# Two unmerged gate units of a feed-forward block become merged ones: predicted and tested

## The chip, the cores and the metric

The program runs on one core of one Trainium2 chip. The core has five engines that run side by side, each through its own list of instructions in a fixed order: TensorE (PE: matrix products, with weight loads, PEld, that overlap them), VectorE (DVE), ScalarE (ACT), GpSimd (POOL) and SyncE (SP, which issues DMAs). An instruction that has to wait for another engine holds up everything behind it on its own engine. The metric is the device time of one execution in microseconds; less is better.

## The reference

One layer: a modulated input goes through a token mixer (windowed attention and retention, gated and projected), a layer norm, and then through the part that the change is in, a feed-forward block with a short convolution over the 256 tokens. All in float32, sequence 256, width 1024, hidden width 2816:

```python
def conv_ffn(h, w_ff_gate, w_ff_up, ff_conv_w, ff_conv_b, w_ff_down):
    s = h.shape[1]
    g = h @ w_ff_gate
    u = h @ w_ff_up
    gp = jnp.pad(g, ((0, 0), (CONV_WIDTH - 1, 0), (0, 0)))
    g_conv = sum(gp[:, j:j + s, :] * ff_conv_w[j] for j in range(CONV_WIDTH)) + ff_conv_b
    a = jax.nn.gelu(g_conv, approximate=False) * u
    return a @ w_ff_down
```

A second layer norm follows.

## The kernel before, in words

**Precision.** A float32 value is split in two parts, hi and lo, and a product is the sum of three: hi by hi, hi by lo, lo by hi. A weight unit is 128x2048 float32, loaded by one DMA into one of four `raw` buffers and split in two halves of 128x1024: ScalarE casts a half into `whi` (L1338), VectorE subtracts (L1352) and gives `wlo`; eight buffers each. The DMA for a later unit waits until the subtraction has read the `raw` buffer.

**Steps.** The main part is a list of steps, two per weight unit as a rule, whose order is that in which the units are written down. At each step the builder emits the splits of the halves that come some halves later, then whatever was put off to this step (`put_off(n, ...)` means n steps later), and then the step's own products and what follows them at once. So the order on every engine is fixed when the program is built.

**The feed-forward block.** The hidden width is cut into 11 rounds of 256. The up products of rounds 0 and 1 are made first, in one group with tokens on the partitions; they are copied to `u4` (L795), transposed on TensorE into banks 6 and 7 (L800, called by `first` in the middle of gate 0) and copied to `uT` (L801). Then come the units gate 0, gate 1, gate 2, up 2, down 0, down 1, gate 3, up 3, down 2, gate 4, and so on. A gate or up unit gives 256 hidden columns of 256 tokens, as two halves of 128 columns. There are two kinds:

- *Unmerged* (`wstat8`, gates 0 and 1): per half 8 k-tiles by three products of 256 columns (L123, L124, L125), both halves in one PSUM bank of 512 columns, which sums all three. `gate_done` then runs once per unit: first taps with the bias on ScalarE (L814, twice), the other two taps on VectorE straight from PSUM (L817, four times), Gelu (L819), and at once `act_in`: product with up (L860) and the split of the result into hi and lo (L100, L101), which are the operands of the down unit.
- *Merged* (`wstat8m`, all others): h's hi and lo parts lie side by side, so that one product of 512 columns (L134) does whi by both, and one of 256 (L138) does wlo by hi. Each half has a bank of its own. The bank's two column halves have to be added afterwards: ScalarE copies the second to an SBUF slot (L489), and one step later VectorE adds the first to it (L492). The bank is free after that addition. For a gate all three taps follow on VectorE from SBUF (L836, then L838 twice), and Gelu one step later (L841). For an up the product with the gate follows (L848) and the split one and two steps later.

**Banks.** There are eight PSUM banks, P0 to P7. Gate and up units take the next of P0 to P3 in turn (`one_bank`). The down units sum in P4 to P7 until the end.

**Order inside a merged unit.** The first step makes 8 products of 512 into the first bank, then the first product of 512 into the second bank, then 8 of 256 into the first bank. The second step makes 8 of 256 and 7 of 512 into the second bank.

## Time and profile before

| what | value |
|---|---|
| median of 3 runs | 421.58 us (421.49 to 421.66) |
| the profiled execution | 421.43 us |
| its span, first to last instruction | 419.7 us |
| TensorE, matrix products | 412.5 us busy, 98% of the span |
| VectorE | 368.1 us, 88% |
| ScalarE | 248.5 us, 59% |
| mean granted TensorE clock | 0.997 |

The execution takes 1.7 us more than its span. Rows of the timeline give start and length in us of instructions or of runs of equal ones (xN), and in brackets how long the engine stood idle before and what ended that. The length of a run goes from the start of its first to the end of its last; on ScalarE and VectorE an instruction starts about 0.1 us before the one ahead of it ends, so the distance of two starts is what an instruction costs its engine in a run. In the chain of waits the end of the program is followed back from instruction to instruction through what released each.

### The profile page before, as it was taken

The page shows a single profiled execution, that of the slowest core. Times are in us where ns is not written, and L with a number is a line of the kernel's source. Part 1 is how long each engine was busy: PE and PEld are TensorE (multiplying, and loading weights), DVE is VectorE, ACT ScalarE, POOL GpSimd, SP SyncE. Part 2 cuts the span into 40 slices and gives each one's busy share as a digit, 9 for nine tenths or more (in the row PEclk, how much of TensorE's full clock was granted, in tenths as well). Part 3 has the DMA queues.
Part 4 walks back from the last instruction along what each step waited for, and adds up shares of the span by engine and source line. Part 5 has one row for each costly group of instructions (what it writes and reads, how often), then busy time and mean ns, then how long its engine had stood idle before and what let it go on. Part 6 is the DMA issues. An engine that isn't in the chain of part 4 may idle for free.

```text
span 419.7 us, 5879 instructions
## 1 busy us (share of the span) xinstructions
PE 412.5 (98%) x2140; PEld 348.1 (83%) x2140; DVE 368.1 (88%) x597; ACT 248.5 (59%) x410; POOL 14.0 (3%) x26
## 2 busy tenths in 40 slices
PE   7999999999999999999999999999999999999995
PEld 4888888888878888888888898888888888888884
DVE  6889799969998889899887987999999888789996
ACT  5666568787955587535544886555555545455700
POOL 0000000100001000001000001000000010003200
PEclk9999999999999999999999999999999999999998
DMA  8998997685688768789662094985866777450002
GB/s 298 405 410 328 414 404 302 247 324 208 222 308 328 254 244 346 304 319 341 223 269 101 1 361 169 373 295 189 307 260 215 281 284 242 187 198 2 1 6 97
DMA packets 18541, 105.60 MB, mean 252 GB/s; under 512 B 2256, under 2 KB 3536, under 8 KB 7760
## 3 DMA queue, kind: packets, MB, share of 16 engines
q1 hardware_dynamic: 16992, 99.70, 63.1%
q0 software_dynamic: 1376, 4.99, 3.5%
q10 hardware_dynamic: 144, 0.52, 0.5%
q8 instruction: 17, 0.28, 0.3%
q14 instruction: 12, 0.10, 0.1%
HBM read 104.15 MB, written 1.06 MB: 251 GB/s over the span
## 4 chain that ended last, share of the span: by engine, by line
PE 97%; DVE 1%; DMA 1%; issue 0%; DVEq 0%; ACT 0%; ACTq 0%
PE P L134 19%; PE P L123 15%; PE P L124 15%; PE P L125 15%; PE P L329 13%; PE P L138 10%; DMA raw<-in_m 1%; PE P L731 1%; PE P L734 1%; PE P L733 1%; PE P L1125 1%; PE P L1231 1%; PE P L1147 1%; PE P L1171 1%; DVE unread L266 1%; PE P L675 0%
## 5 line engine op out<-in xcount | busy, mean ns | idle before, releaser
L1352 DVE TENSOR_TENSOR wlo<-raw,whi 128x1024 fp32r<-128x1024 f32 x118 | 141.9, 1220 | 14.0 <-ACT whi L1338 13.8
L1338 ACT ACTIVATE whi<-raw 128x1024 fp32r<-128x1024 f32 x118 | 122.1, 1056 | 39.3 <-DMA raw<-in_wpr 10.6
L123 PE MATMUL P<-whi,AH 128*128 128x512 f32 x128 | 50.6, 395 | 0.0
L125 PE MATMUL P<-whi,AH 128*128 128x512 f32 x128 | 49.9, 390 | 0.0
L124 PE MATMUL P<-wlo,AH 128*128 128x512 f32 x128 | 49.8, 389 | 0.0
L329 PE MATMUL P<-whi,AH 128*128 128x512 f32 x160 | 41.7, 391 | 1.1 <-DVE AH L295 1.1
L134 PE MATMUL P<-AYa,whi 128*128 128x512 f32 x144 | 41.7, 391 | 0.0
L255 DVE CUSTOM_DVE_ANT_0 junk<-raw,srow 128x1024 bf16<-128x1024 f32 x32 | 39.0, 1219 | 0.0
L134 PE MATMUL P<-AYb,whi 128*128 128x512 f32 x144 | 38.7, 390 | 0.0
L329 PEld LDWEIGHTS P<-whi,AH 128*128 128x128 f32 x160 | 29.8, 188 | 8.4 <-ACT whi L312 1.9
L489 ACT ACTIVATE A<-P 128x256 f32<-128x256 f32 x36 | 13.7, 381 | 33.9 <-PE P L138 23.6
L134 PEld LDWEIGHTS P<-AYb,whi 128*128 128x128 f32 x144 | 27.0, 188 | 6.0
L312 ACT ACTIVATE whi<-raw 128x512 fp32r<-128x512 f32 (+1 forms) x26 | 20.8, 824 | 17.7 <-DMA raw<-in_b 16.3
L134 PEld LDWEIGHTS P<-AYa,whi 128*128 128x128 f32 x144 | 25.8, 189 | 4.2
L315 DVE TENSOR_TENSOR wlo<-raw,whi 128x512 fp32r<-128x512 f32 (+1 forms) x26 | 23.5, 936 | 6.2 <-ACT whi L312 5.8
L123 PEld LDWEIGHTS P<-whi,AH 128*128 128x128 f32 x128 | 24.0, 188 | 5.2 <-issue 0.3
L125 PEld LDWEIGHTS P<-whi,AH 128*128 128x128 f32 x128 | 24.0, 188 | 5.1
L124 PEld LDWEIGHTS P<-wlo,AH 128*128 128x128 f32 x128 | 24.1, 188 | 4.8
L329 PE MATMUL P<-wlo,AH 128*128 128x512 f32 x80 | 23.2, 390 | 0.0
L138 PE MATMUL P<-AYb,wlo 128*128 128x256 f32 x144 | 23.1, 283 | 0.0
L138 PE MATMUL P<-AYa,wlo 128*128 128x256 f32 x144 | 23.0, 282 | 0.0
L138 PEld LDWEIGHTS P<-AYa,wlo 128*128 128x128 f32 x144 | 20.9, 190 | 1.4
(323 smaller groups left out, 776.1 us busy)
## 6 DMA issues: line engine op xcount, KB each, us to landing
raw<-in_ada SPq DMA_DIRECT2D x16, 1024.0 KB, 5.1
raw<-in_wup SPq DMA_DIRECT2D x11, 1024.0 KB, 5.7
raw<-in_wgate SPq DMA_DIRECT2D x11, 1024.0 KB, 5.7
raw<-in_wdown SPq DMA_DIRECT2D x11, 1024.0 KB, 4.9
raw<-in_winB SPq DMA_DIRECT2D x6, 1024.0 KB, 6.8
raw<-in_m SPq DMA_DIRECT2D x4, 1024.0 KB, 8.3
raw<-in_b SPq DMA_DIRECT2D x4, 1024.0 KB, 7.2
raw<-in_wrot SPq DMA_DIRECT2D x4, 1024.0 KB, 7.4
```

Of the source, the lines that this page charges most:

```text
L123: pe.matmul(o, lh, rh, start=start, stop=False)
L124: pe.matmul(o, lh, rl, start=False, stop=False)
L125: pe.matmul(o, ll, rh, start=False, stop=stop)
L134: pe.matmul(banks()[half], t[0][:, k * 128:(k + 1) * 128], x2(k), start=k == 0, stop=half > 0 and k == 7)
L138: pe.matmul(banks()[half][:, :256], t[1][:, k * 128:(k + 1) * 128], x2(k)[:, 0], start=False, stop=half == 0 and k == 7)
L255: dve.tensor_tensor_reduce(out=nobody(j if own else None), in0=raw, in1=srow, scale=1.0, scalar=0.0, op0=OP.mult, op1=OP.add, accum_out=mo ...
L312: act.activation(hi[:, o], raw[:, o], AF.Copy)
L315: dve.tensor_tensor(lo[:, o], raw[:, o], f(hi[:, o]), OP.subtract)
L329: pe.matmul(pa[b0 + c // 512 * 2 + t], x[xi][:, j, t * 128:(t + 1) * 128], ws[k][:, c:c + 512], start=first and (xi, k) == (0, 0), stop=la ...
L489: act.activation(t, p[:, 256:], AF.Copy)
L1338: act.activation(hi, src, AF.Copy)
L1352: dve.tensor_tensor(lo, src, f(hi), OP.subtract)
```

## The change

Gates 0 and 1 become merged units, and the unmerged kind goes. What follows differs a little from the other merged gates: the first tap of the first half is made on ScalarE (from the SBUF slot, L806 in the changed kernel), and the other two taps of that half are put off one step. The product with up and the split (`act_in`) are put off two steps after the second half's taps, and Gelu one step. The transposes of `uT` stay between the two halves of gate 0. The line that set the bank counter back to 0 inside gate 0 goes.

```diff
-MERGED = 2
+XROWS = 2
-    def merged(src, x2, done):
+    def merged(src, x2, done, mid=None):
...
         def two(ts):
+            if mid:
+                mid()
             low(ts[0], 1)
             high(ts[0], 1, range(1, 8))
             done(1, banks()[1])
...
-    def wstat8(name, u, xh, xl, done, mid=None):
...
-    def gate_done(r):
...
     def gate_done_m(r):
         def fn(half):
             g, x = gu(r)[:, half], gu(r)[:, 2 + half]
             convw = consts["convw"]
             w = lambda n: convw[:, n, 2 * r + half:2 * r + half + 1]
-            dve.tensor_scalar(g, x, w(2), w(3), op0=OP.mult, op1=OP.add)
-            for n in (1, 0):
-                dve.scalar_tensor_tensor(g[:, 2 - n:], x[:, :254 + n], w(n), g[:, 2 - n:],
-                                         op0=OP.mult, op1=OP.add)
+            early = r < XROWS and half == 0
+            if early:
+                act.activation(g, x, AF.Identity, scale=w(2), bias=w(3))
+            else:
+                dve.tensor_scalar(g, x, w(2), w(3), op0=OP.mult, op1=OP.add)
+
+            def taps():
+                for n in (1, 0):
+                    dve.scalar_tensor_tensor(g[:, 2 - n:], x[:, :254 + n], w(n), g[:, 2 - n:],
+                                             op0=OP.mult, op1=OP.add)
+            if early:
+                put_off(1, taps)
+            else:
+                taps()
             if half:
                 put_off(1, lambda: act.activation(gu(r)[:, :2], gu(r)[:, :2], AF.Gelu))
+                if r < XROWS:
+                    put_off(2, lambda: act_in(r))
         return fn
...
-    def act_in(r, u):
...
+    def act_in(r):
+        g = gu(r)[:, :2]
+        dve.tensor_tensor(g, S["uT"][:, 2 * r:2 * r + 2], g, OP.mult)
+        ah, al = S["a", r] = a_slots(r)
+        split(ah, al, g)
...
     def first():
-        bank_i[0] = 0
         for t in range(2):
             up_T(t)
 
-    wstat8("wgate", 0, gh2, gl2, gate_done(0), first)
+    ffn_gate(0, first)
     ffn_gate(1)
```

How the instructions stand on three engines, in lists that give line, operation, output and operands. The number behind a tile's name is that of its allocation, so that P3_2270 is bank 3 as gate 0 uses it and P3_2398 the same bank as gate 2 uses it; A5 and A15 are the slots of the rounds in turn; raw_2203 is the unit down 0, raw_2211 down 1, raw_2251 gate 3.

ScalarE before, from the last cast of up 2 on. The first cast of down 0 (from raw_2203) is followed by the copies to uT, gate 0's taps and Gelu, the hi part of the result (A9a), and only then the other halves of down 0 and down 1:

```order
L1338 ACTIVATE whi_2253<-raw_2026 128x1024
L1338 ACTIVATE whi_2294<-raw_2203 128x1024
L801 ACTIVATE AH_2193<-P6_2298 128x4x128
L801 ACTIVATE AH_2193<-P7_2304 128x4x128
L814 ACTIVATE A5_2334<-P2_2269,tables_592 128x256 x2
L819 ACTIVATE A5_2334<-A5_2334 128x512
L100 ACTIVATE A9a_2343<-A5_2334 128x512
L1338 ACTIVATE whi_2347<-raw_2203 128x1024
L1338 ACTIVATE whi_2378<-raw_2211 128x1024
```

ScalarE now, from the same place to the Gelu of gate 0:

```order
L1307 ACTIVATE whi_2253<-raw_2026 128x1024
L475 ACTIVATE A5_2288<-P2_2269 128x256
L1307 ACTIVATE whi_2290<-raw_2203 128x1024
L806 ACTIVATE A5_2288<-A5_2288,tables_592 128x256
L787 ACTIVATE AH_2193<-P6_2296 128x4x128
L787 ACTIVATE AH_2193<-P7_2302 128x4x128
L475 ACTIVATE A5_2288<-P3_2270 128x256
L1307 ACTIVATE whi_2324<-raw_2203 128x1024
L475 ACTIVATE A15_2355<-P0_2336 128x256
L1307 ACTIVATE whi_2357<-raw_2211 128x1024
L819 ACTIVATE A5_2288<-A5_2288 128x512
```

The tap of gate 0's first half (L806) now stands ahead of the two uT copies, of the copy of gate 0's second half and of the cast of down 0's second half; it reads what VectorE's addition writes.

VectorE before, from the first subtraction of down 0 on; the taps read the banks themselves:

```order
L1352 TENSOR_TENSOR wlo_2296<-raw_2203,whi_2294 128x1024
L817 SCALAR_TENSOR_TENSOR A5_2334<-P2_2269,tables_592,A5_2334 128x255 x2
L817 SCALAR_TENSOR_TENSOR A5_2334<-P2_2269,tables_592,A5_2334 128x254 x2
L860 TENSOR_TENSOR A5_2334<-AH_2193,A5_2334 128x512
L101 TENSOR_TENSOR A2a_2344<-A5_2334,A9a_2343 128x512
L1352 TENSOR_TENSOR wlo_2349<-raw_2203,whi_2347 128x1024
L1352 TENSOR_TENSOR wlo_2380<-raw_2211,whi_2378 128x1024
```

VectorE now, from the same place to the first addition of gate 1:

```order
L1321 TENSOR_TENSOR wlo_2292<-raw_2203,whi_2290 128x1024
L478 TENSOR_TENSOR A5_2288<-P2_2269,A5_2288 128x256
L1321 TENSOR_TENSOR wlo_2326<-raw_2203,whi_2324 128x1024
L812 SCALAR_TENSOR_TENSOR A5_2288<-A5_2288,tables_592 128x255
L812 SCALAR_TENSOR_TENSOR A5_2288<-A5_2288,tables_592 128x254
L478 TENSOR_TENSOR A5_2288<-P3_2270,A5_2288 128x256
L808 TENSOR_SCALAR A5_2288<-A5_2288,tables_592 128x256
L812 SCALAR_TENSOR_TENSOR A5_2288<-A5_2288,tables_592 128x255
L812 SCALAR_TENSOR_TENSOR A5_2288<-A5_2288,tables_592 128x254
L1321 TENSOR_TENSOR wlo_2359<-raw_2211,whi_2357 128x1024
L478 TENSOR_TENSOR A15_2355<-P0_2336,A15_2355 128x256
```

The subtraction of down 0's second half now stands between the two additions of gate 0. After the last row shown come the second subtraction of down 1, the product with up and the split of gate 0, the two put-off taps of gate 1's first half, and then the addition of its second half.

TensorE now, the end of gate 1, gate 2 and the start of up 2, with what an instruction waits for in brackets:

```order
L134 MATMUL P1_2337<-AYb_1546,whi_2205 128x512 x4
L134 MATMUL P2_2397<-AYa_1545,whi_2241 128x512 [waits DVE_49,Activation_49]
L134 MATMUL P2_2397<-AYa_1545,whi_2241 128x512 x3
L134 MATMUL P2_2397<-AYb_1546,whi_2241 128x512 x4
L134 MATMUL P3_2398<-AYa_1545,whi_2243 128x512 [waits DVE_49,Activation_49]
L138 MATMUL P2_2397<-AYa_1545,wlo_2245 128x256 x4
L134 MATMUL P0_2458<-AYa_1545,whi_2247 128x512 [waits DVE_49,Activation_49]
L134 MATMUL P0_2458<-AYb_1546,whi_2247 128x512 x4
L134 MATMUL P1_2459<-AYa_1545,whi_2253 128x512 [waits DVE_49,Activation_49]
```

Some rows between are left out. Before, gate 0 had P2 alone, gate 1 P0 alone, gate 2 P1 and P2, up 2 P3 and P0; now gate 0 has P2 and P3, gate 1 P0 and P1, gate 2 P2 and P3 again, up 2 P0 and P1 again.

## The prediction

> **What bounds the kernel now.** The first page gives the busy shares and the chain of waits by engine.

> ```profile
> span 419.7 us, 5879 instructions
> PE 412.5 (98%) x2140; PEld 348.1 (83%) x2140; DVE 368.1 (88%) x597; ACT 248.5 (59%) x410; POOL 14.0 (3%) x26
> PE 97%; DVE 1%; DMA 1%; issue 0%; DVEq 0%; ACT 0%; ACTq 0%
> ```

> 97% of the chain is TensorE. So only two things move the end: fewer or shorter products, and a new wait of TensorE. I then cut the time into stages (columns: length, then busy time and count of PE, PEld, DVE, ACT, POOL, granted clock, DMA share, GB/s): gates 0 and 1, gate 2 and up 2, down 0 and 1, and the rounds after.

> ```profile
> 240.00:252.50 12.50, 12.50 (x106) 12.46 (x105) 10.70 (x13) 10.02 (x14) 0.00 (x0) 1.00 0.87 324
> 252.50:263.70 11.20, 11.20 (x67) 9.88 (x66) 8.53 (x13) 8.08 (x12) 2.08 (x4) 1.00 0.50 164
> 263.70:280.00 16.30, 16.30 (x81) 13.83 (x80) 15.51 (x22) 8.94 (x12) 0.00 (x0) 1.00 0.94 343
> 280.00:310.00 30.00, 30.00 (x158) 25.80 (x157) 29.50 (x48) 15.20 (x22) 0.00 (x0) 1.00 0.66 236
> ```

> TensorE never stands still here, at full clock. VectorE has 4.5 us to spare in the first two stages and next to none later. What the change adds to it falls into the first two, and must be done by the time TensorE needs a bank or an operand. So I looked for those times in the timeline of TensorE.

> ```profile
> 240.14 0.28 PE L123 MATMUL P<-AYa,whi 128*128 128x256 f32 x1
> 243.01 1.03 PE L800 MATMUL P<-ident,AH 128*128 128x128 f32 x8
> 252.51 1.09 PE L134 MATMUL P<-AYa,whi 128*128 128x512 f32 x4
> 254.35 0.39 PE L134 MATMUL P<-AYa,whi 128*128 128x512 f32 x1
> 254.58 0.64 PE L138 MATMUL P<-AYa,wlo 128*128 128x256 f32 x4
> 256.49 0.86 PE L134 MATMUL P<-AYa,whi 128*128 128x512 f32 x3
> 258.11 1.07 PE L134 MATMUL P<-AYa,whi 128*128 128x512 f32 x4
> 263.67 0.39 PE L123 MATMUL P<-whi,A9a 128*128 128x512 f32 x1
> 269.11 0.39 PE L123 MATMUL P<-whi,A9b 128*128 128x512 f32 x1
> 274.55 1.07 PE L134 MATMUL P<-AYa,whi 128*128 128x512 f32 x4
> ```

> The starts are what counts: gate 0 at 240.14, gate 2 at 252.51 and its second bank at 254.35, up 2 at 258.11, down 0 at 263.67, down 1 at 269.11, gate 3 at 274.55.

> **The products.** From 240.14 to 252.51 are 12.37 us: 8 transposes and 96 products of 256 columns, which leave 0.120 each after 0.87 for the transposes. A merged unit costs 258.11 - 252.51 = 5.60 with the bank changes, a little less inside (16 by 0.228 and 16 by 0.1195 are 5.56). Two are 11.15 against 11.50. Gain: 0.35 us, 0.08%. Same columns, fewer instructions; even without any new wait this is less than the 0.2% that a measurement of this kernel can tell from no change.

> **The work for VectorE and ScalarE.** Their rows in this stretch:

> ```profile
> 242.70 4.84 ACT L1338 ACTIVATE whi<-raw 128x1024 fp32r<-128x1024 f32 x5
> 247.44 1.06 ACT L801 ACTIVATE AH<-P 128x512 f32<-128x512 f32 x2
> 258.23 0.63 ACT L819 ACTIVATE A<-A 128x512 f32<-128x512 f32 x1 [2.20 <-DVE A L817]
> 259.62 0.63 ACT L100 ACTIVATE A9b<-A 128x512 fp32r<-128x512 f32 x1 [0.76 <-DVE A L860]
> 261.10 0.36 ACT L489 ACTIVATE A<-P 128x256 f32<-128x256 f32 x1
> 261.37 1.05 ACT L1338 ACTIVATE whi<-raw 128x1024 fp32r<-128x1024 f32 x1
> L300 ACT ACTIVATE A7a<-AYa,mod 128x256 f32<-128x256 f32 x4 | 2.3, 587 | 0.0
> ```

> ```profile
> 243.78 5.77 DVE L1352 TENSOR_TENSOR wlo<-raw,whi 128x1024 fp32r<-128x1024 f32 x5 [1.05 <-ACT whi L1338]
> 249.47 1.64 DVE L817 SCALAR_TENSOR_TENSOR A<-P,tables,A 128x255 f32<-128x255 f32 x4
> 258.89 0.69 DVE L860 TENSOR_TENSOR A<-AH,A 128x512 f32<-128x512 f32 x1 [0.76 <-ACT A L819]
> 260.28 0.69 DVE L101 TENSOR_TENSOR A2b<-A,A9b 128x512 fp32r<-128x512 f32 x1 [0.70 <-ACT A9b L100]
> 261.23 2.44 DVE L1352 TENSOR_TENSOR wlo<-raw,whi 128x1024 fp32r<-128x1024 f32 x2 [0.26 <-ACT whi L1338]
> 263.59 0.42 DVE L492 TENSOR_TENSOR A<-P,A 128x256 f32<-128x256 f32 x1
> 264.05 0.41 DVE L836 TENSOR_SCALAR A<-A,tables 128x256 f32<-128x256 f32 x1
> 264.50 1.00 DVE L838 SCALAR_TENSOR_TENSOR A<-A,tables 128x255 f32<-128x255 f32 x2
> 265.42 1.22 DVE L1352 TENSOR_TENSOR wlo<-raw,whi 128x1024 fp32r<-128x1024 f32 x1
> ```

> Per instruction, from start to start: a cast 0.95, a copy of 256 columns 0.27, a uT copy 0.50, a subtraction 1.13; an addition 0.45 where the next instruction needs its result (0.36 otherwise), a VectorE tap 0.46, a product with up 0.61. Next after a result of the other engine: 0.03. The tap on ScalarE from SBUF has no row; the nearest are L300 (0.587, same size, from SBUF) and, for the bound below, a plain copy (0.36). I take 0.59 to the result and 0.50 to the next start; 0.2 either way, twice.

> Per gate VectorE gets two additions and one first tap, and its four taps in dependent pairs (1.84) where the old ones ran interleaved in 1.64: 0.9 + 0.45 + 0.2, so 3.1 us for both. That would fit in the 4.5 to spare, but the order decides, and so I laid the new orders end to end. (The same laying of the old order puts the Gelu of gate 1 at 258.22; its row says 258.23.)

> *Gate 0.* ScalarE's first four casts are out at 246.50, as in the row; then the copy of the first half (246.50), the first cast of down 0 (246.77 to 247.82). Next stands the tap, which needs VectorE's addition. VectorE is at its five subtractions until 249.43, so the addition is done at 249.85. ScalarE stands still for 2.2 us, and behind the tap on it are both uT copies, the copy of gate 0's second half and the second cast of down 0. These go out one after another: 249.88, 250.38, 250.88, 251.38, 251.65; the cast is ready at 252.70. VectorE's next instruction is the subtraction of just this cast: 2.9 us idle. It runs 252.73 to 253.86, two taps follow, and gate 0's second addition is done at **255.23**.

> TensorE by then is at gate 2. Gate 2 starts at 252.51 - 0.35 = 252.16, and asks for its second bank 8 products later, 254.0 (as 252.51 to 254.35 in the rows). That bank is P3, in which gate 0's second half lies. First wait: 255.3 - 254.0, **1.4 us** with the restart.

> *Gate 1.* VectorE: three taps of gate 0's second half, a subtraction of down 1 (256.66), the first addition of gate 1 (done 258.21). ScalarE meanwhile waits for the Gelu's operand (256.77) and then for this addition: tap 258.24, copy of the second half 258.74, second cast of down 1 259.01 to 260.06. VectorE waits 1.9 for it, subtracts until 261.22, multiplies by up, waits 0.8 for ScalarE's hi part (261.94 to 262.57), subtracts again (262.60), makes the two put-off taps (263.21 and 263.70), and the second addition of gate 1 is done at **264.58**.

> TensorE asks for that bank, P1, as up 2's second: up 2 starts at 252.16 + 1.4 + 5.56 = 259.1, asks at 260.9. Second wait: 264.7 - 260.9, **3.8 us**.

> **Sum.** 1.4 + 3.8 - 0.35 = 4.8 us. Down 0 starts at 268.5 instead of 263.67; its operands from gate 0 are there (263.3). Down 1 starts at 273.9; its last operand is done at 272.2, a cover of 1.7. If that were gone, TensorE would wait there too. Gate 3 starts at 279.35, 4.8 late, and its banks are free (additions of gate 2 at 267.6 and 272.5). No DMA is added, and the two that wait for the subtractions of down 0 and 1 get theirs at 253.95 and 261.3, where the old order has the last at 262.4 (row 261.23, first of two). VectorE is then about as late as TensorE, so the full rounds after run as before and the shift stays to the end: 421.43 + 4.8 = 426.2 for the profiled execution, and as the median is 0.15 above it, **426.4 us**.

> **Rivals.**

> *The clock falls in the second wait.* The end of the program shows such a fall (timeline, then stages of 1 us; the clock is the third column from the right):

> ```profile
> 414.58 1.12 PE L915 MATMUL P<-A,AYb 128*128 128x512 f32 x2 [0.43 <-ACT AYb L913]
> 416.00:417.00 1.00, 0.00 (x0) 0.00 (x0) 0.67 (x2) 0.00 (x0) 0.00 (x0) 1.00 0.17 68
> 417.00:418.00 1.00, 0.00 (x0) 0.00 (x0) 0.00 (x0) 0.00 (x0) 0.00 (x0) 0.72 0.97 354
> 418.00:419.00 1.00, 0.00 (x0) 0.00 (x0) 0.00 (x0) 0.00 (x0) 0.00 (x0) 0.50 0.29 102
> ```

> The last products end at 415.70; 0.72 for the stage from 417 to 418 means half clock from 417.44, 1.7 us later. A wait of 3.8 us is longer than that, one of 1.4 is not. If half clock then lasts about as long as the wait did, half of 3.6 us of products is lost: 428.2 us. Against it: one fall at the end does not tell whether it counts from the last product or by windows of its own, and with windows a wait may fall across two. [...]

> *Only part of the waits.* Should the tap on ScalarE not hold up the uT copies and casts that long (the addition earlier, the first wait nearly gone), the second would shrink with it: about 3 us in all, 424. Against it stand the five subtractions, which are in the rows as they are.

> *Down 1 waits as well.* Each new handover that costs 0.1 more eats from the cover of 1.7; some twenty lie before it. 1 us beyond gives 427.5.

> *Not slower.* The waits vanish if the second addition of gate 1 is done by 259.5, when TensorE would ask without a first wait. VectorE stands idle 2.9 + 1.9 + 0.8 before it; without these it would be done at 259.0, and only the 0.35 would be left: 421.2. It would take ScalarE doing the casts of down 0 and 1 ahead of the waiting taps. The decisive point is the cast of down 0's second half, which would have to be ready by 249.9. Against it: ScalarE's rows 258.23 and 259.62 show it waiting 2.20 and 0.76 with casts behind.

> **How the numbers follow.** The forecast 0.48, with a range of its own of 425.3 to 427.2 (0.4 below and above for the tap, the rest for handovers); fallen clock 0.34 (427.2 to 428.8); part of the waits 0.09; down 1 as well 0.05; not slower 0.04. The range 425.2 to 428.8 leaves out the two cases below and a little above, under 0.2. Slower has 0.94; of the rest, 0.04 within 0.2% (0.84 us, as the gain alone is 0.35) and 0.02 faster.

> **What would show it.** Right: in the chain VectorE's additions between TensorE's products, twice, at about 255 and 264; on TensorE a wait before the first product of gate 2's and of up 2's second bank, named after the addition; ScalarE idle 2.2 before the first tap; VectorE idle 2.9 and 1.9 before the second casts of down 0 and 1; unit lengths from gate 3 on as before. Wrong: no idle time on TensorE near 254 and 261 (then the order does not bind as I read it), waits named after something else, or a granted clock below 1 after 264, which is the first rival.

## The result and the profile after

| | before | changed kernel |
|---|---|---|
| median | 421.58 us (421.28 to 421.80, 5 executions) | 427.89 us (426.29 to 428.96, 5 executions) |
| the profiled execution | 421.43 us, span 419.7 | 427.89 us, span 426.2 |
| mean granted clock, profiled | 0.997 | 0.995 |

The ratio is 1.0144 (95% interval 1.0128 to 1.0159): slower by 6.3 us, 1.5 more than the 426.4 that was forecast. The first page of the changed kernel and TensorE's waits on VectorE's additions (waited for; us in total, times, longest):

```profile
span 426.2 us, 5822 instructions
PE 414.8 (97%) x2108; PEld 348.1 (82%) x2108; DVE 370.9 (87%) x603; ACT 249.2 (58%) x412; POOL 14.0 (3%) x26
PE 88%; DVE 5%; ACT 3%; issue 1%; DMA 1%; DVEq 0%; ACTq 0%
PE P L134 <- DVE A L478: 4.8, 2, 3.6
```

TensorE's share of the chain of waits fell from 97% to 88%; VectorE and ScalarE have taken 5% and 3%. Its 32 instructions fewer are the products of the two merged gates (64 in place of 96), and the two waits of 4.8 us in all are new. The timeline of TensorE in the changed kernel shows where they are:

```profile
240.18 1.07 PE L134 MATMUL P<-AYa,whi 128*128 128x512 f32 x4
252.17 1.07 PE L134 MATMUL P<-AYa,whi 128*128 128x512 f32 x4
255.41 0.47 PE L134 MATMUL P<-AYa,whi 128*128 128x512 f32 x1 [1.26 <-DVE A L478]
259.24 1.07 PE L134 MATMUL P<-AYa,whi 128*128 128x512 f32 x4
264.79 0.47 PE L134 MATMUL P<-AYa,whi 128*128 128x512 f32 x1 [3.58 <-DVE A L478]
265.75 1.05 PE L138 MATMUL P<-AYb,wlo 128*128 128x256 f32 x4
270.13 0.39 PE L123 MATMUL P<-whi,A9a 128*128 128x512 f32 x1
281.01 1.07 PE L134 MATMUL P<-AYa,whi 128*128 128x512 f32 x4
```

Gate 0 starts at 240.18, gate 2 at 252.17, and the first product of its second bank (P3) waits until 255.41. Up 2 starts at 259.24, and the first product of its second bank (P1) waits until 264.79. After that four products of 256 columns take 1.05 instead of 0.64: that is the other half of the story. In stages (length; PE busy and count, granted clock, DMA share, GB/s):

```profile
265.00:265.50 0.50, 0.50 (x4) 0.82 0.97 410
265.50:268.50 3.00, 3.00 (x16) 0.50 0.04 14
268.50:269.00 0.50, 0.50 (x4) 0.77 0.00 0
```

0.82 in the first half microsecond means half clock from 265.32, 0.77 in the third row half clock until 268.73. So TensorE ran at half clock for 3.41 us, and the fall came only after it was at work again. Down 0 starts at 270.13, gate 3 at 281.01, 6.46 later than the 274.55 of before; the profiled executions differ by 427.89 - 421.43 = 6.46 as well. Nothing is lost or won behind gate 3.

ScalarE of the changed kernel, from the tap of gate 0's first half to that of gate 1's:

```profile
249.96 0.60 ACT L806 ACTIVATE A<-A,tables 128x256 f32<-128x256 f32 x1 [2.11 <-DVE A L478]
250.47 1.06 ACT L787 ACTIVATE AH<-P 128x512 f32<-128x512 f32 x2
...
251.69 1.07 ACT L1307 ACTIVATE whi<-raw 128x1024 fp32r<-128x1024 f32 x1
...
258.33 0.60 ACT L806 ACTIVATE A<-A,tables 128x256 f32<-128x256 f32 x1 [0.85 <-DVE A L478]
```

The tap (L806) waits 2.11 for the addition, and the uT copies, the second half's copy and the cast of down 0's second half go out behind it. VectorE in the same stretch:

```profile
249.51 0.42 DVE L478 TENSOR_TENSOR A<-P,A 128x256 f32<-128x256 f32 x1
252.79 1.23 DVE L1321 TENSOR_TENSOR wlo<-raw,whi 128x1024 fp32r<-128x1024 f32 x1 [2.86 <-ACT whi L1307]
...
254.84 0.42 DVE L478 TENSOR_TENSOR A<-P,A 128x256 f32<-128x256 f32 x1
...
260.18 1.23 DVE L1321 TENSOR_TENSOR wlo<-raw,whi 128x1024 fp32r<-128x1024 f32 x1 [1.89 <-ACT whi L1307]
...
262.70 0.69 DVE L101 TENSOR_TENSOR A2a<-A,A9a 128x512 fp32r<-128x512 f32 x1 [0.70 <-ACT A9a L100]
...
264.23 0.42 DVE L478 TENSOR_TENSOR A<-P,A 128x256 f32<-128x256 f32 x1
...
271.52 0.69 DVE L101 TENSOR_TENSOR A2b<-A,A9b 128x512 fp32r<-128x512 f32 x1 [0.70 <-ACT A9b L100]
```

The two engines hand the turn to and fro, and each stands still while the other works: 2.86, 1.89 and 0.70 on VectorE before the addition at 264.23 that frees P1. The chain of waits (start, length, piece), followed back from 264.79:

```profile
250.47 1.06 ACT AH L787 x2
...
252.79 1.23 DVE wlo L1321
...
258.33 0.60 ACT A L806
...
260.18 1.23 DVE wlo L1321
...
264.31 0.35 DVE A L478
...
264.79 0.47 PE P L134
```

From 250 to 264.79 the chain touches TensorE nowhere. So by this chain the first wait sets nothing by itself: without it, TensorE would only have come earlier to the second.

### The profile page after: what moved, and what is told of

Same layout as the page of the kernel before. It is cut to its first block, busy times and chain, and to the rows that moved or that the text cites. A ratio compares the mean times of both kernels' runs of the same rounds, so it can differ in the third digit from the quotient of the medians.

```text
span 426.2 us, 5822 instructions
## 1 busy us (share of the span) xinstructions
PE 414.8 (97%) x2108; PEld 348.1 (82%) x2108; DVE 370.9 (87%) x603; ACT 249.2 (58%) x412; POOL 14.0 (3%) x26
## 3 DMA queue, kind: packets, MB, share of 16 engines
HBM read 104.15 MB, written 1.06 MB: 247 GB/s over the span
## 4 chain that ended last, share of the span: by engine, by line
PE 88%; DVE 5%; ACT 3%; issue 1%; DMA 1%; DVEq 0%; ACTq 0%
PE P L134 18%; PE P L123 14%; PE P L125 14%; PE P L124 14%; PE P L331 13%; PE P L138 10%; ACT whi L1307 2%; DVE wlo L1321 1%; PE P L1094 1%; PE P L1200 1%; PE P L1116 1%; PE P L1140 1%; DVE unread L268 1%; DMA first<-in_first 1%; DVE A L812 1%
## 5 line engine op out<-in xcount | busy, mean ns | idle before, releaser
L134 PE MATMUL P<-AYa,whi 128*128 128x512 f32 x160 | 46.7, 393 | 4.8 <-DVE A L478 4.8
L123 PE MATMUL P<-whi,AH 128*128 128x512 f32 x128 | 50.6, 395 | 0.0
L134 PE MATMUL P<-AYb,whi 128*128 128x512 f32 x160 | 43.0, 390 | 0.0
L134 PEld LDWEIGHTS P<-AYa,whi 128*128 128x128 f32 x160 | 29.0, 190 | 10.3 <-ACT A L475 4.0
L134 PEld LDWEIGHTS P<-AYb,whi 128*128 128x128 f32 x160 | 30.0, 188 | 6.7
L475 ACT ACTIVATE A<-P 128x256 f32<-128x256 f32 x40 | 15.2, 380 | 33.0 <-PE P L138 23.9
L123 PEld LDWEIGHTS P<-whi,AH 128*128 128x128 f32 x128 | 24.0, 188 | 5.2 <-issue 0.3
L138 PE MATMUL P<-AYb,wlo 128*128 128x256 f32 x160 | 26.5, 290 | 0.0
L138 PE MATMUL P<-AYa,wlo 128*128 128x256 f32 x160 | 26.3, 288 | 0.0
L138 PEld LDWEIGHTS P<-AYa,wlo 128*128 128x128 f32 x160 | 23.8, 195 | 1.5
```

What stands on the lines that cost most here:

```text
L123: pe.matmul(o, lh, rh, start=start, stop=False)
L134: pe.matmul(banks()[half], t[0][:, k * 128:(k + 1) * 128], x2(k), start=k == 0, stop=half > 0 and k == 7)
L138: pe.matmul(banks()[half][:, :256], t[1][:, k * 128:(k + 1) * 128], x2(k)[:, 0], start=False, stop=half == 0 and k == 7)
L475: act.activation(t, p[:, 256:], AF.Copy)
```

## Experiments

The theory: the time comes from the order on ScalarE and VectorE (the waiting tap with the casts behind it), plus half clock after the second wait. The rivals: the load (VectorE simply has too much to do), merged units that are no shorter, and waits that TensorE would have anyway. The first four kernels were timed beside the kernel before at 421.78 us (421.34 to 421.93), the last three beside it at 421.57 us (421.23 to 422.35).

**The tap on VectorE.** ScalarE has nothing to wait for, and VectorE still more to do.

```diff
-            early = r < XROWS and half == 0
+            early = False
```

> The first tap of gate 0's and gate 1's first half goes back from ScalarE to VectorE, with its other two taps right behind it, as in the other merged gates; all else as changed. VectorE has 0.9 us more work than in the changed kernel. Theory order (the waits come from ScalarE standing behind a tap that needs VectorE, with the next cast behind it): both copies and casts go out early, gate 0's second addition is done at 252.9 and TensorE does not wait for bank P3; gate 1's second addition is done at 260.8, TensorE asks at 259.5, one wait of 1.4 us; too short for the clock to fall. 422.6 us, granted clock 0.997 or more. Rival load (VectorE simply has 3.1 us too much): more work, longer waits, 427 us or more. Rival products (the merged gates themselves are slower): no change against the changed kernel, 426.3 to 429.

Measured: 422.68 us (422.39 to 423.42), ratio 1.0025 (1.0015 to 1.0034). TensorE in this kernel:

```profile
261.21 0.47 PE L134 MATMUL P<-AYa,whi 128*128 128x512 f32 x1 [1.23 <-ACT A L475]
```

One wait of 1.23 at up 2's second bank is left, and none at gate 2's. The row names ScalarE's copy of gate 2's first half, whose row ends at 261.20; but that copy reads another bank, and VectorE's addition of gate 1's second half ends at 261.07, 0.14 before the product, as in the changed kernel (264.65 and 264.79). So it is most likely still the addition that the product waits for. 0.9 us over before is left of 6.3, although VectorE does more. The rival load falls.

**The second wait filled.** Fifteen more products of 512 columns in the second wait; they sum in bank 4, and nobody reads the sum.

```diff
             high(ts[0], 0, range(8))
+            spare = bank(4) if fill else None
+            for k in range(fill):
+                pe.matmul(spare, ts[0][0][:, k % 8 * 128:(k % 8 + 1) * 128], x2(k % 8),
+                          start=k == 0, stop=k == fill - 1)
             high(ts[1], 1, range(1))
```

> The changed kernel with 15 extra products of 512 columns into bank P4, which nothing reads, ahead of the first product of up 2's second bank: 15 by 0.2285 are 3.4 us of work inside the wait of 3.6 to 3.8. Theory wait clock (the clock falls because TensorE stands still for 3.6 us in a row): it stays at full rate in every run, 426.2 to 426.7 us in all five, clock 0.998 or more, less spread than the changed kernel's 426.29 to 428.96. Rival other clock (it falls for another reason, or the loss is not the clock's): spread and median stay, about 427.9. If the wait were not there, the extra products would cost 3.4 us: above 429.7.

Measured: 426.5 us (426.14 to 426.79), ratio 1.0114 (1.0099 to 1.0129), with a mean clock of 0.998 to 1.0 in all four executions. TensorE:

```profile
264.55 0.47 PE L134 MATMUL P<-AYa,whi 128*128 128x512 f32 x1 [0.18 <-DVE A L481]
268.38 0.39 PE L123 MATMUL P<-whi,A9a 128*128 128x512 f32 x1
```

The stage of the restart (busy time and count of PE, PEld, DVE, ACT, POOL, then the clock):

```profile
264.00:266.00 2.00, 1.81 (x13) 1.44 (x12) 1.89 (x6) 0.65 (x2) 0.00 (x0) 1.00 0.60 254
```

P1 comes free as late as in the changed kernel, but from the restart to down 0 are 3.83 us where the changed kernel takes 270.13 - 264.79 = 5.34. Products that serve nothing made the program about 1.5 us faster at the median: the clock fall is a cost of its own, and with TensorE kept at work it came in none of the four executions.

**The second wait taken away.** The second half of gate 1 goes to bank 4, which is free until down 0.

```diff
-        banks = lazy(lambda: [one_bank(), one_bank()])
+        def two_of():
+            p = one_bank()
+            if second is None:
+                return [p, one_bank()]
+            bank_i[0] = (bank_i[0] + 1) % 4
+            return [p, bank(second)]
+        banks = lazy(two_of)
```

(`second` is 4 for gate 1 alone.)

> The changed kernel, but gate 1's second half goes to bank P4 instead of P1, so that up 2 finds its second bank free; down 0, which begins P4, is the next to ask. The order of ScalarE and VectorE stays. Theory order: the second wait (3.6) goes, down 0 asks for P4 at 264.7, just after gate 1's second addition at 264.6; but the split of gate 1's result is done at 272.2 only, and down 1 asks for it at 270.1: a new wait of 2.2 there. 1.4 + 2.2 - 0.35 = 3.25: 424.8 us, clock 0.997 or more (0.5 us less would still fit, 1 us more if the clock falls in 2.2). Rival bank (only the bank was short): 1.4 - 0.35, 422.6 us. Rival load or products: as the changed kernel, 426.3 or more.

Measured: 424.27 us (424.23 to 424.40), ratio 1.0062 (1.0047 to 1.0077). TensorE:

```profile
255.41 0.47 PE L141 MATMUL P<-AYa,whi 128*128 128x512 f32 x1 [1.27 <-DVE A L485]
271.54 0.50 PE L123 MATMUL P<-whi,A9b 128*128 128x512 f32 x1 [1.03 <-ACT A9b L100]
277.39 1.07 PE L141 MATMUL P<-AYa,whi 128*128 128x512 f32 x4
```

Up 2 no longer waits, and the lateness of the other two engines shows where the prediction kept its cover: at down 1, which waits 1.03 for ScalarE's hi part. From its first product to gate 3 are 5.85 us instead of the usual 5.44, so some 0.4 more is lost there: the third product, the first to read VectorE's lo part, starts only at 272.27, when the row of that split has ended at 272.21, and the first product after each wait is about 0.1 slower (0.50, at 271.54 and at 272.27, against 0.39 of the others). Of 3.7 us taken away, about 1.4 came back further on. The 2.2 that was expected counted up to the lo part, but the first two products of down 1 read the hi part alone. Two waits of 1.27 and 1.03 us brought no clock fall: the granted clock is 1.00 in every stage from 255 to 259 and from 260 to 276.

**The second wait made longer.** Two instructions on VectorE ahead of gate 1's second addition; their result is read by nobody.

```diff
             def rest():
+                if name == "wgate" and u == 1 and half:
+                    for i in range(2):
+                        dve.tensor_scalar(tmp.tile([128, 1024], mybir.dt.bfloat16, name="junk", bufs=1),
+                                          S["x1"][:, 0], 1.0, None, op0=OP.mult)
                 dve.tensor_tensor(t, p[:, :256], t, OP.add)
```

> The changed kernel with two idle VectorE instructions of 128x1024 (result not read) ahead of gate 1's second addition: 2.26 us more (by the subtractions' 1.13). Theory order: the second wait of TensorE grows by the same 2.26 to 5.9, all of it on the end: 428.6 us where the clock holds. Theory wait clock: 5.9 us of standing still make the clock fall in every run, for about as long as before: 430.0 to 430.6, clock 0.990 to 0.996. Rival cover (something else is the bound there): less than 2 us more than the changed kernel. Rival other clock: as before in some runs at 428.6 and in some above.

Measured: 430.01 us (429.79 to 430.12), ratio 1.0197 (1.0180 to 1.0214). VectorE and TensorE:

```profile
264.22 1.42 DVE L480 TENSOR_SCALAR junk<-A 128x1024 bf16<-128x1024 f32 x2
```

```profile
266.11 0.76 PE L134 MATMUL P<-AYa,whi 128*128 128x512 f32 x1 [4.92 <-DVE A L482]
272.22 0.40 PE L123 MATMUL P<-whi,A9a 128*128 128x512 f32 x1
```

The stages in which its clock changes (columns as with the changed kernel; it stands at 0.50 in all between):

```profile
264.00:264.50 0.50, 0.00 (x0) 0.86 0.93 393
...
271.00:271.50 0.50, 0.50 (x3) 0.81 0.00 0
```

The total was as expected, but not its parts. The two instructions took 1.42 us together, and not the 2.26 I had taken from a subtraction of the same size, so the wait was 4.92 and not 5.9. The clock made up for it: 0.86 and 0.81 give half clock from 264.36 to 271.19, that is 6.83 us, twice 3.41. Its last 5.1 us lay on products, and from the restart to down 0 are 6.11 instead of 3.83. All four executions have a mean clock of 0.992.

**The tap put off by one step.** Same instructions on the same engines as in the changed kernel; the first tap of gate 0 and that of gate 1 both move.

```diff
-                act.activation(g, x, AF.Identity, scale=w(2), bias=w(3))
+                put_off(1, lambda: act.activation(g, x, AF.Identity, scale=w(2), bias=w(3)))
```

> The same instructions on the same engines as in the changed kernel; the first tap of gate 0's and of gate 1's first half stays on ScalarE, but is put off one step, so that the uT copies, the copy of the second half and the cast of down 0's (down 1's) second half stand ahead of it. Theory (the place of the tap in ScalarE's order makes the waits): laid end to end, the wait at gate 2's second bank (P3) is gone, one wait of about 1.1 us is left before the first product of up 2's second bank, gate 3 starts at 275.3 instead of 274.55 before: about 422.3 us, with clock 1 throughout. Rival (the tap is bad on ScalarE wherever it stands, or the extra work of both engines does not fit): waits at both banks as in the changed kernel, 426 us or more.

Measured: 422.53 us (422.03 to 422.80), ratio 1.0020 (1.0011 to 1.0029). ScalarE at gate 0, then TensorE's only wait in the stretch:

```profile
249.10 1.07 ACT L1307 ACTIVATE whi<-raw 128x1024 fp32r<-128x1024 f32 x1
250.09 0.60 ACT L806 ACTIVATE A<-A,tables 128x256 f32<-128x256 f32 x1
```

```profile
260.77 0.47 PE L134 MATMUL P<-AYa,whi 128*128 128x512 f32 x1 [0.92 <-DVE A L478]
```

The tap itself runs at 250.09, as late as in the changed kernel (249.96); only what stood behind it now stands ahead, and the cast of down 0 goes out at 249.10 instead of 251.69. At gate 1 the same is done with the cast of down 1, and the two moves together are worth 5.8 us (428.33 for the changed kernel timed beside it, below), the clock's part included. This is the experiment that separates the place of the tap from the tap.

**No wait at all.** The tap on VectorE, the product with up in slots of its own with its split a step later, and in three steps the casts behind what was put off.

```diff
-            early = r < XROWS and half == 0
+            early = False
...
-        dve.tensor_tensor(g, S["uT"][:, 2 * r:2 * r + 2], g, OP.mult)
+        m = slot(("8a", "8b")[r], [128, 2, 256])
+        dve.tensor_tensor(m, S["uT"][:, 2 * r:2 * r + 2], g, OP.mult)
         ah, al = S["a", r] = a_slots(r)
-        split(ah, al, g)
+        put_off(1, lambda: act.activation(ah, m, AF.Copy))
+        put_off(1, lambda: dve.tensor_tensor(al, m, f(ah), OP.subtract))
...
-        if not late:
+        if not late and not 60 < s < 64:
```

> The change with three things moved: the first tap on VectorE; the product with up of rounds 0 and 1 in slots of its own, with its hi part and lo part one step later; in three steps beside gate 2 and up 2 the splits of weights stand behind what was put off instead of ahead of it. Theory (only the order makes the waits, and the products are 0.35 us shorter): laid end to end no wait on TensorE from gate 0 to gate 3, down 0 at 263.3, down 1 at 268.7, gate 3 at 274.2 (before 274.55): 421.2 us, ratio 0.999. Rival 1 (a wait of 0.5 to 1.2 us comes back at some bank or at a down unit): 421.7 to 422.5. Rival 2 (the merged units are not shorter than the unmerged ones on the chip): 421.6, as before.

Measured: 421.33 us (421.05 to 422.48), ratio 0.9994 (0.9985 to 1.0003). TensorE:

```profile
240.35 1.07 PE L134 MATMUL P<-AYa,whi 128*128 128x512 f32 x4
252.34 1.07 PE L134 MATMUL P<-AYa,whi 128*128 128x512 f32 x4
274.44 1.07 PE L134 MATMUL P<-AYa,whi 128*128 128x512 f32 x4
```

From gate 0 to gate 2 are 11.99 us (before 252.51 - 240.14 = 12.37) and to gate 3 34.09 (before 34.41), with no wait between. So the merged units are shorter, by about 0.35, as the trace tells. As a time of the whole program it can't be told from no change: the interval holds 1, and this kernel doesn't beat the one before by what can be measured.

**The changed kernel again**, for more executions (its text is the same).

> The changed kernel itself, for more executions. Theory (the waits are the same in each, 1.3 and 3.6 us, and the clock falls after the second in some of them): single times between 426.2 and 427.0 where it does not fall, and 427.8 to 429.0 where it does, few in between; median 426.5 to 428.5. Rival (the time over the forecast is in longer waits of TensorE in some executions, not in the clock): times over 427.5 with a mean granted clock as high as in the short ones.

Measured: 428.33 us (427.54 to 429.76, four executions), ratio 1.0161 (1.0141 to 1.0181). The profiled execution, 427.54 us: TensorE, then the clock in stages:

```profile
255.30 0.47 PE L134 MATMUL P<-AYa,whi 128*128 128x512 f32 x1 [1.28 <-DVE A L478]
264.68 0.77 PE L134 MATMUL P<-AYa,whi 128*128 128x512 f32 x1 [3.58 <-DVE A L478]
269.77 0.39 PE L123 MATMUL P<-whi,A9a 128*128 128x512 f32 x1
```

```profile
264.00:264.50 0.50, 0.00 (x0) 0.63 1.00 426
264.50:267.50 3.00, 2.82 (x12) 0.50 0.32 131
267.50:268.00 0.50, 0.50 (x6) 0.95 0.00 0
```

The waits are the same to 0.02 us. The half clock lasts from 264.13 to 267.55, again 3.42 us, but began 1.19 earlier in the program, so that 0.55 of it lay in the wait: restart to down 0 takes 5.09, against 5.34 and, without a fall, 3.83. All nine executions of the changed kernel, by mean granted clock:

| clock | times, us | spans, us |
|---|---|---|
| 0.999 | 426.29, 426.92 | 424.6, 424.9 |
| 0.995 to 0.996 | 427.54, 427.89, 427.89, 428.12, 428.55 | 425.8 to 426.6 |
| 0.992 | 428.96, 429.76 | 427.2, 428.0 |

3.41 us at half clock are 0.5 x 3.41 / 426 = 0.004 of the mean clock, twice that 0.008: so the three rows fit none, one and two such periods. (The mean of every execution also contains what of the fall at the program's end lies inside its span, up to 0.003, as in the profile of the kernel before: 0.997.) The rival of longer waits falls, since the longer times are those with the lower clock. My two groups were too few: 427.54 lies below the upper one and 429.76 above it.

## Why the prediction was right, and where it was not

- **The products.** Predicted gain 0.35. Gate 0's start to gate 2's: 11.99 against 12.37, 0.38; to gate 3 without waits 0.32. Right.
- **The tap's price.** Taken as 0.59 to the result and 0.50 to the next start. Measured 0.60, and 250.47 - 249.96 = 0.51. Right.
- **Gate 0.** ScalarE idle 2.2 before the tap: 2.11. VectorE idle 2.9 before the subtraction of down 0's second half: 2.86. First wait 1.4, counted from when the product would have come: gate 2's start plus the 1.84 of before is 254.01, and it came at 255.41, 1.40. Right.
- **Gate 1.** VectorE idle 1.9 and 0.8: 1.89 and 0.70. The second addition was laid out to be done at 264.58; its row ends at 264.23 + 0.42 = 264.65. Second wait 3.8: 264.79 - (259.24 + 1.84) = 3.7. Right to 0.1.
- **Down 1 and what follows.** Its last operand was to be there at 272.2: 271.52 + 0.69 = 272.21. Down 1 did not wait. That the cover is no more than the way to this operand, the kernel with bank 4 shows: there down 1 came at 270.5, and it waited. Right, and the shift stayed to the end.
- **The clock.** This is where the forecast missed. Down 0 was laid out for 268.5 and came at 270.13. The step that failed is the choice between the forecast, with 0.48, and the first rival, with 0.34: by the mean clock the fall came in seven of nine executions, and the median lies in that rival. The range holds because it reaches over that rival too; the forecast value itself was 1.5 too low. The rival's price, half of 3.6 us, was a little high: restart to down 0 was 1.3 and 1.5 longer in the two profiled executions. I had argued that half clock lasts about as long as the wait did; in the three profiles it lasted 3.41 and 3.42 after a wait of 3.58, and 6.83 after one of 4.92. The third shows that the length doesn't follow the wait; that the first two are near it says nothing more. The two executions without a fall, 426.29 and 426.92, are near the forecast.
- **The other rivals.** "Only part of the waits" falls: both were whole. "Not slower" did not happen, but its condition was the right one. It asked for the casts of down 0 and 1 ahead of the waiting tap; put there, they leave 422.53. The kernel with no wait at all, in which VectorE does not stand idle from gate 0's first addition to gate 1's second, takes 421.33, against the 421.2 that was worked out; it also has the tap on VectorE.

## What to carry to other kernels

An instruction that waits for another engine can cost far more than its own duration, through what stands behind it in its list: moving the same two taps on the same engine one step later was worth 5.8 us. Lay the lists of all engines end to end from measured durations, also for work far from the engine that sets the end; that gave each idle time in the changed kernel to 0.1 us. Where such a layout leaves the matrix engine idle for some microseconds, add the price of half clock (in three profiles the way from the restart to down 0 took 1.3, 1.5 and 2.3 us more than the 3.83 without a fall) with a chance that grows with the wait: here it came in no execution at 1.3, in most at 3.6, in all at 4.9.

## What the runs showed of the hardware

```profile
425.50:426.00 0.50, 0.00 (x0) 0.74 0.00 0
424.50:425.00 0.50, 0.00 (x0) 0.56 0.00 0
```

That is half clock from 425.74 and from 424.56, 160.42 and 160.43 us after the first fall. In the changed kernel the granted clock is 0.70 from 265.31 to 265.33 and 0.72 from 268.72 to 268.74, which puts the ends of the first half clock at 265.318 and 268.731: 3.413 us. Both distances are 47 times that. So in each of the two executions both falls lie on one grid, with over 150 us of work between them. In the second execution both falls stood 1.2 us earlier, while the span was 0.4 shorter (425.8 against 426.2). And the same wait of 3.58 us cost 5.34 from the restart to down 0 in the one execution and 5.09 in the other.

**How much of 3.41 us was busy when the clock changed, and when it did not.** A window is taken here as the 3.41 us that end or begin with a change of the clock. The window that ended with the fall at 265.32 held 0.53 us of products after the restart (264.79 to 265.32), and the one that ended at 417.44 in the kernel before held 1.24. In the kernel with the longer wait, the window from 264.36 to 267.77 held 1.66 us of products and did not bring the full clock back (length, PE busy and count, clock, DMA share, GB/s; the kernel before, then the longer wait):

```profile
414.03:417.44 3.41, 1.24 (x3) 1.00 0.18 70
264.36:267.77 3.41, 1.66 (x7) 0.50 0.35 149
```

But the 2.87 us of products in the window of the repeated changed kernel (264.68 to 267.55) did. So falls came after windows that were 16% and 36% busy, no return after one of 49%, a return after one of 84%. These four windows fit a share of busy time that decides; whether it does, where between these the limit lies, and whether it is one limit for both, no run shows. It would also explain the two executions without a fall, with the wait of 3.58 us cut into two windows of which neither was idle enough (cut in the middle, each would be 48% busy), and those with two periods; that is my estimate from these shares, since none of these executions left a profile.

**A VectorE instruction with one source** (128x1024 float32 to bf16, both in SBUF) took (1.42 - 0.1) / 2 = 0.66 us, with 0.1 for the overlap at its end; the subtraction of the same size, with two sources, takes 1.13. The two also differ in operation and output type, so the rows don't show that the second source is the cause.
